# A streaming encoder layer on eight cores: later weights copied to bf16 in the first pass, third-pass buffers laid over early freed ones, engine orders from forward and backward list schedules

## The chip, the cores and the metric

The kernel runs on the 8 cores of one Trainium2 chip. Every core works on its own share of the data: half of one prompt stream (4096 rows), a halo of 128 rows before it, and 64 rows of new frames of running streams. The cores do not talk to each other. The metric is the device time of the slowest core, in microseconds (us). Repeated executions agree within a few tenths of a per cent, except in a second, slower state, in which some executions of any 8-core program fall. Engine names: PE is TensorE (PEld its weight loads), DVE is VectorE, ACT is ScalarE, POOL is GpSimd, and SP issues DMAs. PSUM (`PS` in the traces) is where this kernel's matmuls write; it is used as 8 banks.

## The reference, cut to what matters

```python
def encoder_layer(x, ...):
    x = x + 0.5 * swiglu_ffn(x, g_ff1, w_ff1_in, w_ff1_out)     # first pass  ("A" in the traces)
    z = rms_norm(x, g_mix) @ w_in                               # second pass ("B")
    cv, cg, q, k, v = split(z)
    c_out = conv_tail(history + cv * sigmoid(cg), w_dw, ...)    # causal depthwise conv, layer norm, swish
    a_out = attention(rope(norm(q)), rope(norm(k)), v, sinks)   # own chunk and the two before
    x = x + concat(c_out, a_out) @ w_out
    x = x + 0.5 * swiglu_ffn(x, g_ff2, w_ff2_in, w_ff2_out)     # third pass  ("C")
```

The model width is 1024, the hidden width of both feed-forward blocks 2816 (22 tiles of 128). All weights arrive as float32.

## The kernel before

The kernel records all its operations in program order together with what they read and write (on-chip buffers in pieces of 64 bytes, PSUM in banks), derives the dependencies, and lets a small scheduler choose an order for each engine. Each engine then runs its list strictly in order; semaphores enforce the dependencies. A dependency follows program order: if two operations use one buffer, the one recorded first goes first, and no scheduler can turn that round.

The scheduler before is greedy: an engine takes, among its next 24 operations, the first that is ready.

```python
WINDOW = {"sync": 24, "scalar": 24, "vector": 24, "gpsimd": 24, "tensor": 24}
def pick(e):
    ...                                  # cut: walks the engine's queue from its head
        if r <= f: return (f, u)         # the first one in program order that is ready
```

First and third pass are the same class: blocks of 384 rows; an up-projection writes `H`, a down-projection reads it. Weights are cast from float32 by the DMA itself.

```python
self.WU = C([128, NJ, 2048], BF16, "wu")     # lowest addresses: up weights, then down weights,
self.WD = C([128, NJ, 1024], BF16, "wd")     # then H, normed rows (XNT), rows (XA, XR) ...
def load_w(self, j): self.O.dma("gpsimd", ..., self.WU[:, j, :], self.wu[j])      # float32 -> bf16
def prologue():
    step = conv_weights(K, A.wd_off + 15 * 2048)   # its buffers lie over the last down weights
    for j in range(NJ): A.load_w(j)
    for g in range(16): step(g)                    # VectorE builds, a DMA stores: 16 x 288 KB
    for j in range(NJ): A.load_d(j)
```

The second pass runs in steps of 128 rows. This is the program order of a step, with the PSUM banks that each part uses:

```python
for n in range(last_step):
    flush_late()                              # ends normalization of step n-1's q, k (writes QN)
    if proj: self.glu_pe(n); self.glu_act(n)  # banks 0, 1
    if att:  self.transp(trq, ...)            # bank 6: q, k of step n-1 transposed
    ...                                       # cut: statistics, GLU product, convolution (banks 6, 7)
    if att:  self.scores(n - 1, 0)            # banks 2, 3, then an exponential on ScalarE
    if att:  self.scores(n - 1, 1)            # banks 4, 5
    if proj: self.qkv_pe(..., (self.pb[2], self.pb[3]))    # banks 2, 3: q, k, v of step n
    if att:  self.pv(n - 1)                   # banks 4, 5
    if proj: trq, f = self.qkv_post(n, ...)   # square, reduce, scale, rotate: ScalarE and VectorE
    ...                                       # cut: output projection of step n-22 (banks 0, 1)
```

## Time and profile before

The median is 2823.14 us. From the page of the slowest core: the busy time of the engines, then 40 equal slices of the span, each digit the busy tenths of a slice; PEclk is the granted TensorE clock and DMA the share of the 16 DMA engines.

```profile
PE 2492.3 (88%) x14740; PEld 1365.4 (48%) x14740; DVE 1032.1 (37%) x2701; ACT 747.9 (27%) x1303; POOL 216.3 (8%) x380
PE   1699999999999998888688962469999999999998
PEclk9899999999999998899799986779999999999999
DMA  9931222112221163223244559862111221111110
```

TensorE is full, except at the start, in the second pass (about slices 16 to 23) and in a deep hole after it. The windows view of the same execution, cut at four events: the end of the first pass's last down matmul, the last attention matmul, the first down matmul of the third pass, and the end. Columns: stretch and length, busy time of PE, PEld, DVE, ACT and POOL with instruction counts, granted clock, DMA share, GB/s.

```profile
0.00:1090.90 1090.90, 1000.79 (x5900) 557.97 (x5901) 405.90 (x1199) 257.50 (x445) 87.21 (x145) 0.98 0.34 86
1090.90:1612.10 521.20, 434.14 (x2747) 218.14 (x2744) 272.38 (x620) 263.38 (x451) 52.75 (x97) 0.91 0.35 98
1612.10:1911.00 298.90, 160.87 (x922) 91.36 (x919) 110.77 (x271) 68.10 (x110) 58.74 (x105) 0.77 0.74 180
1911.00:2817.90 906.90, 896.50 (x5181) 497.88 (x5179) 243.04 (x611) 158.91 (x297) 17.64 (x33) 1.00 0.15 50
```

I call these stretches first pass, inside of the second pass, transition, and rest. TensorE is idle for 90 us, nearly all at the start, then 87, 138 and 10 us. What TensorE waited for (six of its waits in the whole execution; total us, times, longest):

```profile
PE PS L343 <- DVE A_sm L343: 62.6, 2, 36.1
PE PS L343 <- DVE B_mc_145 L343: 51.0, 2, 30.1
PE PS L343 <- DVE B_x_128 L343: 32.9, 3, 26.2
PE PS L343 <- DVE B_qn L343: 28.9, 15, 4.0
PE PS L343 <- DVE B_qkt L343: 21.4, 17, 7.0
PE PS L343 <- DVE C_xb L343: 14.9, 3, 7.8
```

The first is the start (VectorE's row norms). The second and third are the transition: the transposed convolution output `B_mc` and the output buffers `B_x`. The next two are short waits for normed and transposed q and k inside the second pass. The last is for the third pass's own row norms. The chain of waits shows why the transition is long: small DMAs take 25 us while the third pass's float32 weights stream in (start, length, what).

```profile
1736.39 25.41 DMA B_mt_161<-zd
1768.94 26.77 DMA x<-B_x_128
```

### The profile page before, as it was taken

How to read it: one execution, taken by the hardware profiler on the slowest of the kernel's cores; microseconds unless marked ns; L12 is line 12 of the kernel's file. 1: busy time of each engine (PE TensorE's matmuls, PEld its weight loads, DVE VectorE, ACT ScalarE, POOL GpSimd, SP SyncE). 2: the span in 40 equal slices, each digit the busy share in tenths (PEclk: the TensorE clock that was granted, in tenths of full speed). 3: DMA queues.
4: the chain of work that ended last, by engine and by line, in shares of the span. 5: the costliest groups of instructions: out<-in, count | busy, mean ns of one | idle time of the engine just before them, and what ended most of it. 6: DMA issues, size and time to landing. Idle time of an engine off the chain costs nothing.

```text
span 2817.9 us, 41303 instructions; the slowest of 8 cores (2803.6 to 2817.9 us)
## 1 busy us (share of the span) xinstructions
PE 2492.3 (88%) x14740; PEld 1365.4 (48%) x14740; DVE 1032.1 (37%) x2701; ACT 747.9 (27%) x1303; POOL 216.3 (8%) x380
## 2 busy tenths in 40 slices
PE   1699999999999998888688962469999999999998
PEld 0345555555555554334344530145555555555554
DVE  2243443334433333544647562143223332233211
ACT  1112222222222222545546440031112211122110
POOL 2110000000000011000111123110000000000000
PEclk9899999999999998899799986779999999999999
DMA  9931222112221163223244559862111221111110
GB/s 199 165 94 55 76 79 64 47 48 79 87 64 42 38 159 74 55 57 105 68 132 115 184 169 217 197 145 64 45 53 38 68 68 52 53 40 52 46 45 23
DMA packets 111521, 244.00 MB, mean 87 GB/s; under 512 B 32415, under 2 KB 49695, under 8 KB 111319
## 3 DMA queue, kind: packets, MB, share of 16 engines
q0 software_dynamic: 42592, 131.65, 18.4%
q1 hardware_dynamic: 68727, 109.70, 13.5%
q8 instruction: 121, 1.98, 0.3%
q14 instruction: 81, 0.66, 0.1%
HBM read 207.82 MB, written 74.79 MB: 100 GB/s over the span
## 4 chain that ended last, share of the span: by engine, by line
PE 81%; DMA 9%; DVE 4%; issue 3%; ACT 2%; POOL 0%; SPq 0%; DVEq 0%; POOLq 0%; ACTq 0%
PE PS L343 81%; DMA wdc<-W_wb 3%; DMA x<-B_x_128 1%; DMA W_ey<-eye 1%; DMA B_mt_161<-zd 1%; DMA B_mt_160<-zd 1%; DVE B_y L343 1%; DMA C_wu<-wu 0%; ACT B_pt L343 0%; DMA B_x_128<-x 0%; DMA C_xa<-x 0%; DVE W_wb L343 0%; DMA B_hc<-sconv 0%; DVE B_qn L343 0%; ACT B_sq L343 0%
## 5 line engine op out<-in xcount | busy, mean ns | idle before, releaser
L343 PE MATMUL PS<-A_xnt,A_wu 128*128 128x384 bf16 (+1 forms) x3872 | 652.8, 330 | 0.9 <-ACT A_xnt L343 0.9
L343 PE MATMUL PS<-C_xnt,C_wu 128*128 128x384 bf16 (+1 forms) x3872 | 628.5, 324 | 0.8 <-ACT C_xnt L343 0.8
L343 PEld LDWEIGHTS PS<-A_xnt,A_wu 128*128 128x128 bf16 x3872 | 378.0, 98 | 258.1 <-issue 6.4
L343 PEld LDWEIGHTS PS<-C_xnt,C_wu 128*128 128x128 bf16 x3872 | 378.2, 98 | 240.5 <-issue 1.4
L343 PE MATMUL PS<-A_wd,A_h 128*128 128x512 bf16 (+1 forms) x1496 | 329.3, 381 | 5.0 <-DMA A_wd<-wd 5.0
L343 PE MATMUL PS<-C_wd,C_h 128*128 128x512 bf16 (+1 forms) x1452 | 315.3, 379 | 0.0
L343 ACT ACTIVATE C_sa<-PS 128x384 f32<-128x384 f32 (+1 forms) x242 | 117.5, 485 | 706.3 <-PE PS L343 696.0
L343 DVE TENSOR_TENSOR C_h<-PS,C_sa 128x384 bf16<-128x384 f32 (+1 forms) x242 | 133.3, 551 | 345.9 <-PE PS L343 345.1
L343 DVE TENSOR_TENSOR A_h<-PS,A_sa 128x384 bf16<-128x384 f32 (+1 forms) x242 | 136.0, 563 | 308.4 <-PE PS L343 307.6
L343 ACT ACTIVATE A_sa<-PS 128x384 f32<-128x384 f32 (+1 forms) x242 | 119.7, 495 | 430.2 <-PE PS L343 379.9
L343 PEld LDWEIGHTS PS<-A_wd,A_h 128*128 128x128 bf16 (+1 forms) x1496 | 146.7, 98 | 179.4 <-issue 9.1
L343 PEld LDWEIGHTS PS<-C_wd,C_h 128*128 128x128 bf16 (+1 forms) x1452 | 142.4, 98 | 169.9 <-issue 0.4
L343 DVE SCALAR_TENSOR_TENSOR C_xr<-PS,C_xr 128x512 f32<-128x512 f32 (+1 forms) x66 | 45.6, 691 | 281.3 <-PE PS L343 281.3
L343 PE MATMUL PS<-B_xn,B_wi 128*128 128x512 bf16 x512 | 126.5, 398 | 8.5 <-DVE B_t_76 L343 3.4
L343 PE MATMUL PS<-K_t,A_xb 128*128 128x128 bf16 (+1 forms) x544 | 42.9, 224 | 84.1 <-DVE A_sm L343 62.6
L343 PE MATMUL PS<-B_us,B_wr 128*128 128x256 bf16 (+1 forms) x576 | 88.2, 309 | 30.2 <-DVE B_qkt L343 17.6
L343 DVE SCALAR_TENSOR_TENSOR A_xr<-PS,A_xr 128x512 f32<-128x512 f32 (+1 forms) x68 | 46.9, 690 | 163.3 <-PE PS L343 163.1
L343 PE MATMUL PS<-B_wi,B_xn 128*128 128x256 bf16 (+1 forms) x512 | 92.6, 335 | 8.3 <-ACT B_pt L343 8.3
L343 PE MATMUL PS<-B_wo,B_mc_145 128*128 128x512 bf16 x64 | 20.7, 453 | 83.0 <-DVE B_mc_145 L343 51.0
L343 ACT ACTIVATE A_xb<-A_xr 128x1024 bf16<-128x1024 f32 (+1 forms) x34 | 35.8, 1053 | 201.5 <-DVE A_xr L343 201.5
L387 POOL DMA_DIRECT2D yout<-C_xr x33 | 17.6, 535 | 928.2 <-DVE C_xr L343 928.2
L343 ACT ACTIVATE B_pt<-PS 128x1024 bf16<-128x1024 f32 (+1 forms) x68 | 66.1, 984 | 78.6 <-PE PS L343 78.6
(167 smaller groups left out, 2029.4 us busy)
## 6 DMA issues: line engine op xcount, KB each, us to landing
B_wr<-wdc SPq DMA_DIRECT2D x32, 576.0 KB, 5.0
A_xa<-xin SPq DMA_DIRECT2D x33, 512.0 KB, 3.9
A_xr<-xin SPq DMA_DIRECT2D x33, 512.0 KB, 3.6
x<-A_xr POOLq DMA_DIRECT2D x33, 512.0 KB, 3.0
C_xr<-x SPq DMA_DIRECT2D x32, 512.0 KB, 3.7
C_xa<-x SPq DMA_DIRECT2D x32, 512.0 KB, 3.7
yout<-C_xr POOLq DMA_DIRECT2D x32, 512.0 KB, 2.9
A_wu<-wu POOLq DMA_DIRECT2D x22, 512.0 KB, 37.1
```

Of the source, the lines that this page charges most:

```text
L343: o = self.P.add(eng, lambda e: getattr(e, meth)(**kw), r, w, cost=self.cost(eng, meth, kw))
L387: self.P.add(eng, lambda e: e.dma_start(out=out, in_=in_), r, w, lane=lane, rk=rk, wk=wk, cost=1.0 if eng == "gpsimd" else 0.5, nbytes=n * ...
```

## The change

The intent is to close the holes around TensorE by four parts:

1. **Convolution steps moved.** VectorE's building of the convolution weights and their stores leave the start; 32 half-sized steps are spread over the first pass.
2. **Copies.** In the first pass, while DMA is idle, 60 DMAs copy all later weights from float32 to bf16 within DRAM. Later loads then read half the bytes, and can use the sync queue.
3. **Layout.** The third pass's rows, normed rows and `H` and 11 of its 22 up-weight tiles lie over projection and attention buffers, which end early. The other 11 lie over the convolution's. PSUM banks of up- and down-projection are exchanged so that up-projections avoid the banks of the output projection.
4. **List schedule.** The whole program is scheduled forward, with priorities from a backward schedule, in three rounds; the best by its own model is kept.

```diff
-    def schedule(self):                      # greedy, window of 24
+    def schedule(self, rounds=3):
+        def run(before, after, prio, back):  # list schedule over all units, by priority (cut)
+        for i in range(rounds):
+            start, order, t = run(preds, succs, prio, False)
+            if best is None or t < best[0]: best = (t, order)
+            start, _, _ = run(succs, preds, [-(start[u] + cost[u]) for u in range(n)], True)
+            prio = [-(start[u] + cost[u]) for u in range(n)]
...
+        fits = NJ if low is None else (low - c1.off) // 4096
+        self.WU = [(c1 if j < fits else c2)([128, 2048], BF16, "wu") for j in range(NJ)]
-        self.PU = [K.pb[0], K.pb[1], K.pb[2], K.pb[3]]
-        self.PD = [K.pb[4], K.pb[5]]
+        self.PU = [K.pb[2], K.pb[4], K.pb[3], K.pb[5]]
+        self.PD = [K.pb[0], K.pb[1]]
...
+    def hook(bi, j):                         # called in the first pass's up-projection
+        if bi == 0: return
+        if j % 3 == 1 and casts:
+            t, k, dst, src = casts.pop(0)
+            O.dma("gpsimd", "pc%d" % (k % 4), dst, src, wk=[("pc", t, k)], after=P.last["vector"])
+        if j % 5 == 3 and convs: wstep[0](*convs.pop(0))
...
-            O.dma("gpsimd", "bwi%d" % k, self.WI[:, k, :], d.wi[k])
+            O.dma("sync", "bwi%d" % k, self.WI[:, k, :], d.wib[k], rk=[("pc", "wi", k)])
...
-    Cc = FF(K, base, "C", d.wu2, d.wd2, ...)
+    Cc = FF(K, (c0, c0, c2), "C", d.wu2b, d.wd2b, ..., low=M.mid, weng="sync")
```

More of the change, by code (lines that the diff above doesn't have):

```diff
@@ L1 @@
+from heapq import heappush, heappop
 import numpy as np
@@ L15 @@
 SEM_MAX = 30000
+MARGIN = 0.5
+SLACK = 2
 ES = {F32: 4, BF16: 2, I32: 4}
 ATOM = 64
-WINDOW = {"sync": 24, "scalar": 24, "vector": 24, "gpsimd": 24, "tensor": 24}
 class _Op:
@@ L38, in __init__ @@
         self.order = None
+        self.last = {}
+        self.trace = []
     def sbuf(self, name, shape, dt, offset):
@@ L79, in atoms, with add @@
         return r
-    def add(self, eng, fn, reads=(), writes=(), lane=None, rk=(), wk=(), cost=0.1, nbytes=0):
+    def add(self, eng, fn, reads=(), writes=(), lane=None, rk=(), wk=(), cost=0.1, nbytes=0, after=None):
         o = _Op()
@@ L118, in add @@
             rd[k] = {}
+        if after is not None:
+            raw.add(after)
         if lane is not None:
@@ L125, in add @@
         weak.discard(o.idx)
+        self.last[eng] = o.idx
         o.deps = raw | weak
@@ L143, in units @@
         return out
-    def schedule(self):
+    def schedule(self, rounds=3):
         ops, units = self.ops, self.units()
         n = len(units)
-        deps = [set() for _ in range(n)]
+        preds = [set() for _ in range(n)]
         for u, l in enumerate(units):
             for o in l:
-                deps[u].update(ops[d].unit for d in o.deps)
-            deps[u].discard(u)
-        users = [[] for _ in range(n)]
-        left = [len(d) for d in deps]
-        for u, d in enumerate(deps):
+                preds[u].update(ops[d].unit for d in o.deps)
+            preds[u].discard(u)
+        succs = [[] for _ in range(n)]
+        for u, d in enumerate(preds):
@@ L157, in schedule @@
             for x in d:
-                users[x].append(u)
+                succs[x].append(u)
         eng = [l[0].eng for l in units]
-        queue = {e: [u for u in range(n) if eng[u] == e] for e in ENGS}
-        head = {e: 0 for e in ENGS}
-        free = {e: 0.0 for e in ENGS}
-        ready = [0.0] * n
-        done = [False] * n
-        pipe = 0.0
-        order, starts = [], []
-        cand = {}
-        def pick(e):
-            q, h = queue[e], head[e]
-            while h < len(q) and done[q[h]]:
-                h += 1
-            head[e] = h
-            best, bt, seen = None, None, 0
-            f = free[e]
-            while h < len(q) and seen < WINDOW[e]:
-                u = q[h]
-                h += 1
-                if done[u]:
-                    continue
-                seen += 1
-                if left[u]:
-                    continue
-                r = ready[u]
-                if r <= f:
-                    return (f, u)
-                if bt is None or r < bt - 0.05:
-                    best, bt = u, r
-            return None if best is None else (bt, best)
@@ L191, in schedule @@
-        dirty = set(ENGS)
-        for _ in range(n):
-            for e in dirty:
-                cand[e] = pick(e)
-            e = min((x for x in ENGS if cand[x] is not None), key=lambda x: cand[x][0])
-            t, u = cand[e]
-            done[u] = True
-            cost = sum(o.cost for o in units[u])
-            free[e] = end = t + cost
-            if units[u][0].lane is not None:
-                pipe = max(pipe, end + 0.5) + units[u][0].nbytes / 230e3
-                end = max(pipe, end + 1.5) + 0.3
-            order.append(u)
-            starts.append(t)
-            dirty = {e}
-            for x in users[u]:
-                left[x] -= 1
-                lat = 0.06 if eng[x] == e else 0.16
-                if ready[x] < end + lat:
-                    ready[x] = end + lat
-                if not left[x]:
-                    dirty.add(eng[x])
@@ L213, in schedule, with release, pick @@
-        self.order = [o for u in order for o in units[u]]
-        self.model_us = max(free.values())
+        cost = [sum(o.cost for o in l) for l in units]
+        dma = [l[0].lane is not None for l in units]
+        wire = [l[0].nbytes / 250e3 if d else 0.0 for l, d in zip(units, dma)]
+        def run(before, after, prio, back):
+            left = [len(x) for x in before]
+            ready = [0.0] * n
+            free = {e: 0.0 for e in ENGS}
+            wait, now = {e: [] for e in ENGS}, {e: [] for e in ENGS}
+            start = [0.0] * n
+            order = []
+            pipe = 0.0
+            def release(u):
+                heappush(wait[eng[u]], (ready[u], prio[u], u))
+            def pick(e):
+                f, w, r = free[e], wait[e], now[e]
+                while w and w[0][0] <= f + 1e-9:
+                    _, p, u = heappop(w)
+                    heappush(r, (p, u))
+                if r:
+                    return f
+                return w[0][0] if w else None
+            for u in range(n):
+                if not left[u]:
+                    release(u)
+            cand = {e: pick(e) for e in ENGS}
+            for _ in range(n):
+                e = min((x for x in ENGS if cand[x] is not None), key=lambda x: cand[x])
+                t = cand[e]
+                if now[e]:
+                    u = heappop(now[e])[1]
+                else:
+                    u = heappop(wait[e])[2]
+                start[u] = t
+                order.append(u)
+                end = free[e] = t + cost[u]
+                if dma[u] and not back:
+                    pipe = max(pipe, end + 0.5) + wire[u]
+                    end = max(pipe, end + 1.5) + 0.3 + SLACK
+                dirty = {e}
+                for x in after[u]:
+                    left[x] -= 1
+                    lat = 0.06 if eng[x] == e else 0.16 + (MARGIN if back else 0.0)
+                    if back and dma[x]:
+                        lat += 2.0 + SLACK + wire[x]
+                    if ready[x] < end + lat:
+                        ready[x] = end + lat
+                    if not left[x]:
+                        release(x)
+                        dirty.add(eng[x])
+                for x in dirty:
+                    cand[x] = pick(x)
+            return start, order, max(free.values())
@@ new lines, in schedule @@
+        prio = list(range(n))
+        best = None
+        for i in range(rounds):
+            start, order, t = run(preds, succs, prio, False)
+            if best is None or t < best[0]:
+                best = (t, order)
+            start, _, _ = run(succs, preds, [-(start[u] + cost[u]) for u in range(n)], True)
+            prio = [-(start[u] + cost[u]) for u in range(n)]
+            self.trace.append(t)
+        self.order = [o for u in best[1] for o in units[u]]
+        self.model_us = best[0]
@@ L379, in tr, with dma @@
         self.op("tensor", "transpose", out=out, in_=in_, identity=identity)
-    def dma(self, eng, lane, out, in_, rk=(), wk=()):
+    def dma(self, eng, lane, out, in_, rk=(), wk=(), after=None):
         r = [in_] if in_.tensor.name in self.P.info else []
@@ L387, in dma @@
         self.P.add(eng, lambda e: e.dma_start(out=out, in_=in_), r, w, lane=lane, rk=rk, wk=wk,
-                   cost=1.0 if eng == "gpsimd" else 0.5, nbytes=n * max(ES[in_.dtype], ES[out.dtype]))
+                   cost=1.0 if eng == "gpsimd" else 0.5, nbytes=n * max(ES[in_.dtype], ES[out.dtype]), after=after)
 class Carve:
@@ L422, with __init__ @@
 class FF:
-    def __init__(self, K, off, tag, wu, wd, g1, g2, blocks, src, dst, xnd=None, rkey=None, wkey=None, nkey=None):
+    def __init__(self, K, carves, tag, wu, wd, g1, g2, blocks, src, dst, xnd=None, rkey=None, wkey=None, nkey=None, low=None, cwd=None, weng="gpsimd", hook=None):
         self.K, self.O, self.tag = K, K.O, tag
@@ L430, in __init__ @@
         self.rkey, self.wkey, self.nkey = rkey, wkey, nkey
-        C = Carve(K.P, off, tag)
         nmax = max(sum(n for _, n in b) for b in blocks)
-        self.WU = C([128, NJ, 2048], BF16, "wu")
-        self.wd_off = C.off
-        self.WD = C([128, NJ, 1024], BF16, "wd")
-        self.H = C([128, NJ, nmax], BF16, "h")
-        self.XNT = [C([128, 8, nmax], BF16, "xnt") for _ in range(2)]
-        self.XA = [C([128, D], F32, "xa") for _ in range(2)]
-        self.XR = [C([128, D], F32, "xr") for _ in range(3)]
-        self.XB = [C([128, D], BF16, "xb") for _ in range(2)]
-        self.XO = [C([128, 8, 128], BF16, "xo") for _ in range(2)] if g2 is not None else None
-        self.SA = [C([128, nmax], F32, "sa") for _ in range(2)]
-        self.G1 = C([128, D], F32, "g1")
-        self.G2 = C([128, D], F32, "g2") if g2 is not None else None
-        self.SM = C([128, 8, 16], F32, "sm")
-        self.end = C.off
+        self.weng, self.hook = weng, hook
+        c0, c1, c2 = carves
+        self.XA = [c0([128, D], F32, "xa") for _ in range(2)]
+        self.XNT = [c0([128, 8, nmax], BF16, "xnt") for _ in range(2)]
+        self.XB = [c0([128, D], BF16, "xb") for _ in range(2)]
+        self.G1 = c0([128, D], F32, "g1")
+        self.SM = c0([128, 8, 16], F32, "sm")
+        self.SA = [c0([128, nmax], F32, "sa") for _ in range(2)]
+        self.H = c0([128, NJ, nmax], BF16, "h")
+        fits = NJ if low is None else (low - c1.off) // 4096
+        self.WU = [(c1 if j < fits else c2)([128, 2048], BF16, "wu") for j in range(NJ)]
+        c3 = c0 if cwd is None else cwd
+        self.WD = c3([128, NJ, 1024], BF16, "wd")
+        self.XR = [c3([128, D], F32, "xr") for _ in range(3)]
+        self.XO = [c3([128, 8, 128], BF16, "xo") for _ in range(2)] if g2 is not None else None
+        self.G2 = c3([128, D], F32, "g2") if g2 is not None else None
         self.cnt = dict(xa=0, xr=0, xb=0, xo=0, sm=0, ab=0, d=0, t=0)
         self.g1, self.g2 = g1, g2
-        self.PU = [K.pb[0], K.pb[1], K.pb[2], K.pb[3]]
-        self.PD = [K.pb[4], K.pb[5]]
+        self.PU = [K.pb[2], K.pb[4], K.pb[3], K.pb[5]]
+        self.PD = [K.pb[0], K.pb[1]]
         self.PT = [K.pb[6], K.pb[7]]
@@ L465, in load_w @@
     def load_w(self, j):
-        self.O.dma("gpsimd", self.tag + "wu%d" % (j % 8), self.WU[:, j, :], self.wu[j])
+        k = [("pc", self.tag + "u", j)] if self.weng == "sync" else []
+        self.O.dma(self.weng, self.tag + "wu%d" % (j % 8), self.WU[j][:, :], self.wu[j], rk=k)
     def load_d(self, j):
-        self.O.dma("gpsimd", self.tag + "wd%d" % (j % 8), self.WD[:, j, :], self.wd[j])
+        k = [("pc", self.tag + "d", j)] if self.weng == "sync" else []
+        self.O.dma(self.weng, self.tag + "wd%d" % (j % 8), self.WD[:, j, :], self.wd[j], rk=k)
     def load_xa(self, g):
@@ L542, in up @@
             a, b = self.PU[i], self.PU[2 + i]
-            W = self.WU[:, j, :].rearrange("p (k n) -> p k n", k=8)
+            W = self.WU[j][:, :].rearrange("p (k n) -> p k n", k=8)
             for h, ps in ((0, a), (1, b)):
@@ L551, in up @@
             bg(1)
+            if self.hook:
+                self.hook(bi, j)
             if j == 10:
@@ L673, in __init__ @@
         self.V = [C([128, 128], BF16, "v") for _ in range(4)]
+        self.PT = [C([128, 2, 512], BF16, "pt") for _ in range(3)]
+        self.DN = [C([128, 512], F32, "dn") for _ in range(2)]
+        self.mid = C.off
         self.WO = C([128, 8, 1024], BF16, "wo")
@@ L688, in __init__ @@
         self.KS, self.VSO = self.KO, self.VO
-        self.PT = [C([128, 2, 512], BF16, "pt") for _ in range(3)]
-        self.DN = [C([128, 512], F32, "dn") for _ in range(2)]
         self.WR = [C([128, 2, 1152], BF16, "wr") for _ in range(2)]
@@ L745, in setup @@
         for k in range(8):
-            O.dma("gpsimd", "bwo%d" % k, self.WO[:, k, :], d.wo[k])
+            O.dma("sync", "bwo%d" % k, self.WO[:, k, :], d.wob[k], rk=[("pc", "wo", k)])
         O.memset(self.CN[:, 0:1], EPS)
@@ L992, in load_wd @@
         self.O.dma("sync", "bwr%d" % i, self.WR[i][:, :, :], self.d.wdc[2 * q:2 * q + 2].rearrange("g p n -> p g n"),
-                   rk=[("wdc", 2 * q), ("wdc", 2 * q + 1)])
+                   rk=[("wdc", g, h) for g in (2 * q, 2 * q + 1) for h in range(2)])
     def conv_pe(self, t, q, half):
@@ L1284, in window_out_prompt, with conv_weights, step @@
         O.dma("sync", "bpv", d.ovw_p[:, :], self.VO[:, :])
-def conv_weights(K, off):
+def conv_weights(K, C, buf):
     P, O, d = K.P, K.O, K.d
-    C = Carve(P, off, "W")
-    CO = C([128, 16, 36], F32, "co")
-    EY = C([128, 32], F32, "ey")
-    WB = [C([128, 36, 32], BF16, "wb") for _ in range(2)]
-    O.dma("sync", "wco", CO[:, :, :], d.wcoef)
-    O.dma("sync", "wey", EY[:, :], d.eye32)
-    def step(g):
-        w = WB[g % 2]
-        O.tt(w[:, :, :], EY[:, :].unsqueeze(1).to_broadcast([128, 36, 32]), CO[:, g, :].unsqueeze(2).to_broadcast([128, 36, 32]), ALU.mult)
-        O.dma("gpsimd", "wdc%d" % (g % 2), d.wdc[g], w[:, :, :].rearrange("p a b -> p (a b)"), wk=[("wdc", g)])
+    CO = C([128, 16, 36], BF16, "co")
+    EY = C([128, 32], BF16, "ey")
+    O.dma("gpsimd", "wco", CO[:, :, :], d.wcoef)
+    O.dma("gpsimd", "wey", EY[:, :], d.eye32)
+    def step(g, h):
+        w = buf()[:, :, :].rearrange("p a b -> p (a b)")[:, 0:576]
+        O.tt(w.rearrange("p (a b) -> p a b", b=32), EY[:, :].unsqueeze(1).to_broadcast([128, 18, 32]),
+             CO[:, g, 18 * h:18 * h + 18].unsqueeze(2).to_broadcast([128, 18, 32]), ALU.mult)
+        O.dma("gpsimd", "wdc%d" % h, d.wdc[g][:, 576 * h:576 * h + 576], w, wk=[("wdc", g, h)])
     return step
@@ L1330, in build_nc @@
     dram("wdc", [16, 128, 1152], BF16)
+    dram("wib", [8, 128, 1792], BF16)
+    dram("wob", [8, 128, D], BF16)
+    dram("wu2b", [NJ, 128, 2048], BF16)
+    dram("wd2b", [NJ, 128, D], BF16)
     dram("ud", [512, 4, 1032], BF16)
@@ L1354, in xnd @@
         return d.xne[:, :, g[0] - HALF:g[0] - HALF + g[1]]
-    A = FF(K, base, "A", d.wu1, d.wd1, d.gains[0], d.gains[1], [main[0:2] + [halo, samp]] + b3, d.xin, d.x1,
-           xnd=xnd, wkey=lambda g: [("x1", g[0])], nkey=lambda g: [("xn", g[0] // 128)])
+    cu = Carve(P, base, "A")
+    cr = Carve(P, base + NJ * 4096, "A_")
+    casts = [("wi", k, d.wib[k], d.wi[k]) for k in range(8)] + [("wo", k, d.wob[k], d.wo[k]) for k in range(8)]
+    for j in range(NJ):
+        casts += [("Cu", j, d.wu2b[j], d.wu2[j]), ("Cd", j, d.wd2b[j], d.wd2[j])]
+    convs = [(g, h) for g in range(16) for h in range(2)]
+    def hook(bi, j):
+        if bi == 0:
+            return
+        if j % 3 == 1 and casts:
+            t, k, dst, src = casts.pop(0)
+            O.dma("gpsimd", "pc%d" % (k % 4), dst, src, wk=[("pc", t, k)], after=P.last["vector"])
+        if j % 5 == 3 and convs:
+            wstep[0](*convs.pop(0))
+    A = FF(K, (cr, cu, cu), "A", d.wu1, d.wd1, d.gains[0], d.gains[1], [main[0:2] + [halo, samp]] + b3, d.xin, d.x1,
+           xnd=xnd, wkey=lambda g: [("x1", g[0])], nkey=lambda g: [("xn", g[0] // 128)], hook=hook)
+    wstep = [None]
     def loads(F):
@@ L1367, in prologue @@
     def prologue():
-        step = conv_weights(K, A.wd_off + 15 * 2048)
-        for j in range(NJ):
-            A.load_w(j)
-        for g in range(16):
-            step(g)
-        for j in range(NJ):
-            A.load_d(j)
+        loads(A)()
+        wstep[0] = conv_weights(K, cr, lambda: A.XO[A.nxt("xo", 2)])
     A.run(prologue)
+    assert not casts and not convs
     M = Mixer(K, base)
@@ L1379, in build_nc @@
     M.run()
-    Cc = FF(K, base, "C", d.wu2, d.wd2, d.gains[2], None, [main[0:2] + [samp]] + b3, d.x2, d.yout, rkey=lambda g: [("x2", g[0])])
+    c0 = Carve(P, base, "C")
+    c2 = Carve(P, M.US_off, "C_")
+    Cc = FF(K, (c0, c0, c2), "C", d.wu2b, d.wd2b, d.gains[2], None, [main[0:2] + [samp]] + b3, d.x2, d.yout, rkey=lambda g: [("x2", g[0])],
+            low=M.mid, weng="sync")
+    assert c0.off <= M.US_off
     Cc.run(loads(Cc))
@@ L1383, in build_nc @@
     with ExitStack() as st:
-        print(P.model_us, P.emit(st), A.end, M.end, Cc.end)
+        print(P.model_us, P.emit(st), cr.off, M.mid, M.US_off, M.end, c0.off, c2.off)
     return nc
```

## The prediction

> **What bounds it now.** By the slowest core's page TensorE is busy 2492 of 2818 us; the chain of waits is 81% TensorE. The windows view shows 100% busy at clock 1.00 from 216 to 1092 us (first pass, blocks 1 to 10) and from 1883 to 2808 us (third pass). The loss is elsewhere:
>
> 1. Start, 0 to 216 us: 126 us busy. Block 1 starts at 216.6 us. DMA is 97% busy to 62 us with float32 weights cast on the way. VectorE stands in order behind the convolution-weight steps, which wait for their buffers' stores (27.6 us at one time), and TensorE behind VectorE's norm (36 and 26.6 us). Those buffers lie over the last down weights.
> 2. First to second pass, 1092 to 1118 us: some 15 us.
> 3. Second pass, 1108 to 1660 us: 456 busy of 552 us, clock 0.91; many short waits.
> 4. Second to third pass, 1660 to 1858 us: 75 busy of 198 us, clock 0.69, DMA share 0.84. Two waits on the transposed convolution output (51 us) and three on output buffers (33 us); the chain shows small loads of 25 to 27 us beside 34 MB of float32 weights, issued from 1715 us on.
>
> **What the change does.** (1) The convolution steps leave the start: 4.7 MB of stores (about 24 us at the 197 GB/s measured there) and VectorE's stalls go. Weights are down by 110 to 125 us; the third and fourth row tiles still land at about 50 us, so block 0's up-projection (22 x 3.03 us) runs from 62 to 130 us, its down-projection (8 x 4.7 us) to 168 us. Gain 48 us. (2) The 60 DRAM casts (46 MB read, 23 MB written) go where DMA share is 0.24 and TensorE full: free, as are the small VectorE steps. (3) The second pass's input weights come as bf16 by the sync queue: gain 12 us. The Trainium skill, "DMA: Bandwidth & Descriptors", section "SWDGE vs HWDGE vs iDMA", says a cast during DMA is for the gpsimd queue only, so the copies permit this. (4) List scheduling over the whole program instead of a window of 24 should halve the loss inside the second pass: 45 us. (5) Largest: the third pass's activations and 11 of 22 up-weight tiles lie where projection and attention buffers end, and its PSUM banks avoid the output projection's, so its norms and half of block 0's up-projection (23 us) fill the second pass's tail. All down weights still wait for the last output projections: I leave 40 us. Gain 120 us.
>
> **Sum.** First pass ends at 168 + 876 = 1044 us, second starts at 1049; TensorE work of the second at full clock about 485 us (estimate from the first pass's rate), of the third 945 us; losses 50 inside the second, 40 at the transition, 10 at the end, 5 between profile and median: about 2585 us, 8.5% faster.
>
> Prediction 2585 us, 2510 to 2680. Faster by over 2%: 0.95; within: 0.035; slower: 0.015.
>
> **What would show it.** Block 1's first up matmul at 155 to 185 us; first pass 876 us from there; third-pass matmuls among the second's; TensorE idle between last attention and full third pass below 70 us, not 123.
>
> **What would make it wrong.** Orders tuned to a model whose DMA latencies are too short: in-order queues then stall, chiefly sync with weight loads ahead of small ones; casts delaying stores whose buffers the convolution steps share, so VectorE blocks.

## The result, and the profile after

The changed kernel takes 2675.66 us (median of 4, 2675.11 to 2678.91), the kernel before 2823.14 us. The ratio is 0.9482 (95% interval 0.9463 to 0.9500): 5.2% faster. A ratio here is the mean time of one kernel's fast runs over that of the other's fast runs of the same rounds, so not quite the ratio of the medians quoted. The time lies inside the predicted range, at its upper edge, and 91 us above the predicted value. So the change worked, but some 40% of the expected gain is missing, and the question is which part.

The page's lines after:

```profile
PE 2485.1 (93%) x14740; PEld 1367.4 (51%) x14740; DVE 1030.0 (38%) x2717; ACT 764.4 (29%) x1311; POOL 224.7 (8%) x398
PE   1999999999999999798869976799999999999998
PEclk9999999999999999898879988899999999999999
DMA  9943444345433344122235685750121112110110
```

The first slices are fuller and the hole after the second pass is shallower. The second pass (again about slices 16 to 23) looks much as it did. The windows view, cut at the same four events:

```profile
0.00:1053.60 1053.60, 995.90 (x5883) 555.73 (x5884) 402.30 (x1201) 256.40 (x439) 119.01 (x209) 1.00 0.48 111
1053.60:1570.50 516.90, 446.86 (x2875) 232.30 (x2874) 301.86 (x705) 287.50 (x486) 54.16 (x98) 0.91 0.41 115
1570.50:1779.90 209.40, 154.17 (x881) 86.88 (x882) 88.64 (x226) 65.61 (x99) 33.87 (x59) 0.85 0.67 217
1779.90:2677.20 897.30, 888.20 (x5111) 492.48 (x5107) 237.18 (x585) 154.90 (x289) 17.62 (x33) 1.00 0.15 50
```

First pass 37 us shorter, inside of the second pass **4 us**, transition 90 us, rest 10 us (TensorE has 8 us less to do in it: some work had moved ahead): 141 us, the whole difference of the two profiled spans.

The 4 us are a poor measure of the new order, because the stretch ends with the last attention matmul and a scheduler may put that off. The 166 transposes of q and k, the same in both kernels, show it (count, ns, first and last start in us):

```profile
L343 PE MATMUL PS<-K_t,B_qn x166: 188/219/314, 1116.4 to 1603.3; 128*128 128x128 bf16 x161, 64*128 64x64 bf16 x5
L363 PE MATMUL PS<-K_t,B_qn x166: 190/219/314, 1076.2 to 1520.4; 128*128 128x128 bf16 x161, 64*128 64x64 bf16 x5
```

From the first to the last they take 487 us before and 444 us after, with some 110 fewer matmuls of other work between them; but the last attention matmul follows the last transpose by 9 us before and by 50 us after. The stretch after holds 128 more matmuls than the one before. The fairest figure for the order's gain inside is therefore TensorE's idle time, which falls from 87 to 70 us: 17 us. Three waits of TensorE in the inside and the transition:

```profile
PE PS L363 <- DVE B_qn L363: 26.8, 10, 4.3
PE PS L363 <- DVE C_xb L363: 19.8, 2, 10.6
PE PS L363 <- DVE B_mc_164 L363: 9.9, 2, 5.9
```

The 25 us DMAs are gone from the chain of waits, and the waits on `B_mc` fall from 51 to 10 us. The wait for `B_qn` is nearly as it was (26.8 against 28.9 us), that for `B_qkt` falls from 21.4 to 8.1 us. The wait for the third pass's own row norms (`C_xb`), 15 us before, is 20 us now.

Why does the second pass not shorten more? The chain of waits after, at one step (start, length, what):

```profile
1373.61 7.14 PE PS L363 x40
1380.83 0.71 ACT B_sq L363
1381.63 0.82 DVE B_qs L363
1382.45 0.73 DVE B_t_94 L363
...
1384.87 0.83 DVE B_qn L363
1385.83 0.45 PE PS L363 x5
1386.38 0.50 DVE B_qkt L363
1387.01 7.08 PE PS L363 x38
1394.18 0.71 ACT B_sq L363
```

In this step it is a closed loop, 13.4 us from one `B_sq` to the next. TensorE computes scores, then the next projection; ScalarE squares it; VectorE reduces, scales and rotates; TensorE transposes (`x5`); VectorE copies (`B_qkt`); then come the next scores. Scores and projection share PSUM banks 2 and 3, and the program records scores of step n-1 ahead of the projection of step n. So the projection cannot start before these scores are read, and the scores need the end of the previous projection's whole post-processing. The TensorE timeline before shows a similar beat, from its transposes of `B_qn` (start, length, what; in brackets the idle time just before and what ended it):

```profile
1285.74 0.44 PE L343 MATMUL PS<-K_t,B_qn 128*128 128x128 bf16 x5
1299.33 0.44 PE L343 MATMUL PS<-K_t,B_qn 128*128 128x128 bf16 x5
1313.52 0.44 PE L343 MATMUL PS<-K_t,B_qn 128*128 128x128 bf16 x5 [0.37 <-DVE B_qn L343]
```

Before 13.6 to 14.2 us a step; but there TensorE has more work in a step, and two of these three transposes do not wait. After:

```profile
1372.42 0.44 PE L363 MATMUL PS<-K_t,B_qn 128*128 128x128 bf16 x5 [2.83 <-DVE B_qn L363]
1385.83 0.44 PE L363 MATMUL PS<-K_t,B_qn 128*128 128x128 bf16 x5 [1.82 <-DVE B_qn L363]
1399.24 0.69 PE L363 MATMUL PS<-K_t,B_qn 128*128 128x128 bf16 x5 [3.27 <-DVE B_qn L363]
```

In these steps the beat is 13.4 us, hardly less than before, although the list schedule had moved the gated convolution's projections (glu) elsewhere and they hold less work. It is no fixed bound: from 1160 us on, the steps of this trace take between 11.5 and 16.2 us, and in the step shown the exponential had read the scores by 1375.2 us while the projection began only at 1378.0 us, behind matmuls of the convolution and its statistics that the scheduler had put between. What no order can do is take the post-processing out of the loop. The Trainium skill, "Perfetto Trace Analysis", section "Optimization Strategy", says of such repeated equal gaps that they can mean that there isn't enough SBUF or PSUM for the next tile. This trace agrees in part: in these steps the gap of 2 to 3 us returns every 13.4 us, and the resource is a pair of PSUM banks; but the experiment below shows that it is the order of their users that counts here.

### The profile page after: what moved, and what is told of

The parts are those of the page before. It is cut to its first block, busy times and chain, and to the rows that moved or that the text cites. A ratio compares the mean times of both kernels' runs of the same rounds, so it can differ in the third digit from the quotient of the medians.

```text
span 2677.2 us, 41546 instructions; the slowest of 8 cores (2662.2 to 2677.2 us)
## 1 busy us (share of the span) xinstructions
PE 2485.1 (93%) x14740; PEld 1367.4 (51%) x14740; DVE 1030.0 (38%) x2717; ACT 764.4 (29%) x1311; POOL 224.7 (8%) x398
## 4 chain that ended last, share of the span: by engine, by line
PE 85%; DMA 7%; DVE 4%; issue 2%; ACT 1%; DVEq 0%; POOL 0%; ACTq 0%; POOLq 0%; SPq 0%
PE PS L363 85%; DMA A_wd<-wd 4%; DVE B_y L363 1%; DMA B_wr<-wdc 1%; DMA xnt<-A_xo 0%; DMA A_wu<-wu 0%; DMA B_x_152<-x 0%; DVE B_qs L363 0%; DVE C_sm L363 0%; DMA C_xa<-x 0%; ACT B_sq L363 0%; DVE B_t_94 L363 0%; DVE B_qn L363 0%; ACT B_se L363 0%; DMA x<-B_x_152 0%
## 5 line engine op out<-in xcount | busy, mean ns | idle before, releaser
L363 PEld LDWEIGHTS PS<-B_us,B_wr 128*128 128x128 bf16 x576 | 60.2, 109 | 46.6 <-issue 27.2
L363 PEld LDWEIGHTS PS<-B_xn,B_wi 128*128 128x128 bf16 x512 | 48.5, 100 | 61.8 <-issue 15.1
```

The costliest lines, as they stand in the source:

```text
L363: o = self.P.add(eng, lambda e: getattr(e, meth)(**kw), r, w, cost=self.cost(eng, meth, kw))
```

## The experiments

All outputs are right. Medians are of all runs of a kernel; where slow runs are among them, the lowest stands in brackets. Stretches are from the profile of the slowest core. The kernel before took 2825.5 to 2834.3 us (medians) beside them. The runs come from three chips (old_sched, f32_weights, old_layout and only_sched; qkv_early, bf16_gpsimd and slack8; the other five), so differences of less than about 10 us between these groups are not firm. The border between inside and transition, the last attention matmul, moves with the order; read it together with the total.

| kernel | median us | ratio to before | first pass | inside | transition | rest |
|---|---|---|---|---|---|---|
| before | 2823.1 | 1 | 1090.9 | 521.2 | 298.9 | 906.9 |
| changed | 2675.7 | 0.9482 | 1053.6 | 516.9 | 209.4 | 897.3 |
| old_sched | 2740.8 | 0.9682 | 1051.8 | 516.5 | 263.2 | 905.1 |
| f32_weights | 2730.1 | 0.9647 | 1054.2 | 516.1 | 259.2 | 898.8 |
| old_layout | 2728.5 (2727.3) | 0.9640 | 1055.6 | 509.4 | 255.0 | 905.6 |
| only_sched | 2787.2 (2786.7) | 0.9849 | 1091.0 | 508.4 | 280.3 | 905.6 |
| bf16_gpsimd | 2681.5 (2680.1) | 0.9494 | 1053.0 | 516.8 | 214.3 | 898.5 |
| slack8 | 2736.5 (2722.0) | 0.9670 | 1055.0 | 545.9 | 220.7 | 898.5 |
| qkv_early | 2625.7 (2622.0) | 0.9289 | 1053.4 | 470.4 | 202.9 | 897.2 |
| old_sched_qkv | 2677.5 (2676.6) | 0.9485 | 1053.0 | 455.7 | 261.0 | 905.2 |
| norm_late | 2615.8 | 0.9262 | 1053.3 | 474.2 | 191.5 | 897.4 |
| tiles_first | 2627.8 (2626.2) | 0.9302 | 1055.3 | 476.5 | 196.3 | 897.3 |
| late_slack1 | 2628.4 (2624.6) | 0.9272 | 1057.1 | 484.8 | 188.1 | 897.4 |
| late_slack4 | 2624.4 | 0.9268 | 1055.7 | 465.2 | 202.3 | 897.3 |

### What each part is worth

**old_sched: the changed kernel with the old scheduler.**

```diff
-    def schedule(self, rounds=3):     # list schedule
+    def schedule(self):               # the greedy one of the kernel before, window 24
```

> The changed kernel with the old greedy scheduler (window of 24 units) put back; copies, layout and moved convolution steps stay. Theory: the moved convolution steps alone make the start, so block 1's first up matmul stays at 165 to 185 us; without the list schedule the other gains shrink: first to second pass gap 10 us more, second pass inside 20 to 40 us longer, third-pass matmuls not mixed into the second pass's tail (window too short), so the transition costs 40 us more. Total about 2750 us. Rival: the copies and the layout do nearly all of it and the order little, total below 2700 us. If the start falls back beyond 200 us, the order and not the moved steps made the start.

Measured: 65 us slower than the changed kernel. The first pass stays at 1052 us, so the moved convolution steps made the start, not the order. The inside is the same to half a microsecond, 516.5 us, but this does not refute the theory's 20 to 40 us for it: by the weight loads counted there, the greedy order has 138 fewer matmuls in it, and its q and k transposes take 490 us from first to last, against 444 us. The transition is 54 us longer.

**f32_weights: no copies.**

```diff
-            O.dma("sync", "bwi%d" % k, self.WI[:, k, :], d.wib[k], ...)
+            O.dma("gpsimd", "bwi%d" % k, self.WI[:, k, :], d.wi[k])      # likewise wo, wu2, wd2
+    casts = []
```

> The changed kernel without the bf16 copies: no casts in the first pass, the later weights are read as float32 and cast on the gpsimd queue as before. Theory: first pass unchanged within 5 us (copies are free there); first to second pass gap 10 us longer; transition 15 to 30 us longer because twice the bytes are read where DMA is at 0.7 to 0.9. Total about 2705 us. Rival: the halved bytes are what shortened the transition, then total above 2740 us. If the copies were not free in the first pass, it gets shorter than 881 us here.

Measured: 54 us slower, 50 of them in the transition. This is above my estimate of 15 to 30 us; the total lies between the theory's 2705 us and the rival's 2740 us, nearer to the rival. The first pass is 1054.2 us without copies and 1053.6 us with them: the 60 copies are free there. The second pass does not start later with float32 input weights (inside 516.1 us), so the predicted gain of 12 us at that border does not exist.

**old_layout: the third pass's buffers in the old places.**

```diff
-    Cc = FF(K, (c0, c0, c2), "C", ..., low=M.mid, weng="sync")
+    Cc = FF(K, (c0, c1, c1), "C", ..., cwd=cw, weng="sync")   # c1: bottom, cw above it, c0 on top
```

> The changed kernel with the third pass's buffers laid out as before (up weights at the bottom, then down weights, activations on top); everything else stays. Theory: layout plus whole-program order make the overlap; here activations lie over buffers that live to the end of the second pass, so no third-pass matmul runs before the last output projection or shortly before, and the transition costs 50 to 70 us more: about 2735 us. Rival: layout is of little use because the last output projections bound the transition anyway: below 2700 us. The first pass and the second up to the last attention step stay as in the changed kernel.

Measured: 53 us slower; the transition takes 46 us more. The first up matmul of the third pass starts at 1767 us, after the last output projection at 1726 us; in the changed kernel it starts at 1635 us, 105 us before the last one. As the theory expected. The exchange of the PSUM banks stayed in this run; what it is worth alone was not tested.

**only_sched: the kernel before with the new scheduler alone.**

```diff
-    def schedule(self):               # greedy
+    def schedule(self, rounds=3):     # list schedule
```

> The kernel before with only the scheduler exchanged. Theory: the start stays late (the convolution steps' stores still compete for DMA and their buffers lie under the last down weights; block 1 at 195 to 215 us), the second pass gains 30 to 40 us inside, the transition stays long with float32 loads (100 us or more idle): total about 2765 us. Rival: the order is most of the change: below 2720 us.

Measured: 36 us faster than before by the medians, 1.5% by the ratio. (Its interval, 0.9784 to 0.9913, leaves it open whether that is 2%.) The first pass stays at 1091 us, the inside shortens by 13 us and the transition by 19 us. Order alone helps little where buffers and bytes are in the way.

Taken together: in the transition, taking away any one of order, copies and layout loses 46 to 54 us of the 90 us gained, and order alone gives 19 us (for the order, part of it belongs to the inside, since the order moves the border). The three need each other; their parts do not add up.

**bf16_gpsimd: copies kept, but loaded by the other queue.**

```diff
-            low=M.mid, weng="sync")
+            low=M.mid, weng="gpsimd")       # still from wu2b, wd2b
```

> The changed kernel with the copies kept, but the third pass's bf16 weights loaded by the gpsimd queue instead of the sync queue. Without copies the transition (last attention matmul to first third-pass down matmul) took 259 us, with them 209. Theory bytes: half the bytes make the difference, so it stays at 210 to 220 us, total 2675 to 2690 us. Rival queue: what counts is that the loads leave the gpsimd queue, where they wait in order with the stores and small loads of the tail, then 240 us or more, total above 2710 us.

Measured: 2681.5 us, transition 214 us. Of the 50 us which the copies are worth there, 5 come from the queue of the third pass's weights (less than is firm between groups of runs) and some 45 remain for the bytes. A load of float32 is also cast on the way, and the runs do not separate the halved bytes from the missing cast.

### Why the second pass did not shorten

**qkv_early: the projection recorded ahead of the previous step's scores.**

```diff
+            prev = trq
+            if proj:
+                self.qkv_pe(..., (self.pb[2], self.pb[3]))
+                trq, f = self.qkv_post(n, ...)
...
             if att:
-                self.transp(trq, 128, self.QKT[n % 4])
+                self.transp(prev, 128, self.QKT[n % 4])
...
-            if proj: self.qkv_pe(..., (self.pb[2], self.pb[3]))      # was here, behind the scores
-            if proj: trq, f = self.qkv_post(n, ...)
```

No instruction is added or removed; only who goes first on banks 2 and 3 changes.

> The changed kernel with one edit in the second pass's program: a step's q, k, v projection (and its post-processing) is emitted ahead of the previous step's scores, which share PSUM banks 2 and 3 with it, instead of behind them. Theory: the list schedule did not shorten the second pass (517 against 521 us from its start to the last attention matmul) because the program order of the two users of these banks closes a loop of 13.4 us per step (projection, square, reduce, scale, transpose, scores, exponential, next projection) that no order can break; with the edit the loop loses the square-to-transpose part, 5 to 6 us, steps become bound by TensorE at about 11 to 12 us, this stretch falls to 450 to 475 us, the whole to 2615 to 2640 us. Rival: the stretch is bound by in-order queues or by the low granted clock of 0.91, then it stays above 505 us and the total at 2665 to 2685 us.

Measured: 2625.7 us, 50 us faster than the changed kernel; inside 470.4 us. The wait for `B_qn` is gone from the longest waits, and in its most even steps the transposes follow each other at 11.4 us (mean over all steps 12.4 us, against 14.3 us in the changed kernel and 15.7 us in the one before). From the TensorE timeline:

```profile
1229.55 0.45 PE L363 MATMUL PS<-K_t,B_qn 128*128 128x128 bf16 x5
1240.94 0.46 PE L363 MATMUL PS<-K_t,B_qn 128*128 128x128 bf16 x5
```

and the windows view of the inside:

```profile
1053.40:1523.80 470.40, 428.34 (x2891) 225.92 (x2890) 304.60 (x708) 285.69 (x489) 53.38 (x99) 0.95 0.46 130
```

From 1150 to 1250 us TensorE is now busy all the time at clock 1.00: these steps are bound by it, as the theory had it. TensorE's idle time inside falls from 70 to 42 us, and its busy time for about the same work from 447 to 428 us, because the granted clock rises from 0.91 to 0.95. The rival, a bound by queues or by the clock itself, is refuted: the stretch fell well below its 505 us, and the clock rose as the idle time fell. (Giving the projection other banks, instead of the other order, was not tried.)

**old_sched_qkv: the same edit with the old greedy scheduler.**

```diff
-    def schedule(self, rounds=3):     # list schedule
+    def schedule(self):               # greedy, window 24; with the edit of qkv_early
```

> The early projection with the old greedy scheduler (window of 24). With the old program order the two schedulers took 516 us each from the end of the first pass to the last attention matmul. Theory: the loop over banks 2 and 3 was the bound for either, so here too this stretch falls, to 470 to 495 us, total 2695 to 2720 us. Rival: only the whole-program order can use the freedom, then it stays above 508 us, total above 2730 us.

Measured: inside 455.7 us (516.5 before the edit), even below the expected band, total 2677.5 us. The edit is worth 63 us in total with the greedy scheduler and 50 us with the list schedule: the loop held both back. With this edit of a few lines the old scheduler is as fast as the changed kernel with its new one. With the edit in both, the list schedule is still 52 us ahead in total. The stretches put all of this into the transition, but the list schedule's q and k transposes also take less time from first to last (386 against 422 us), so part of it is won inside.

### The transition

**slack8: the scheduler's model with a larger allowance per DMA.**

```diff
-SLACK = 2
+SLACK = 8
```

> The changed kernel with the model's allowance per DMA raised from 2 to 8 us. Theory: TensorE stands 26 us in the transition (1587 to 1626 us) behind a weight load of the convolution and behind third-pass norms whose row loads came later than the model had them; with a larger allowance these waits shrink by half or more, total 2655 to 2668 us. Rival: the waits come from order on VectorE and ScalarE, not from DMA latencies: within 5 us of the changed kernel, or slower.

Measured: 61 us *slower* by the medians, 29 of them inside the second pass and 11 in the transition by the profiled run, which is one of the quicker ones. Both the theory and its rival's "within 5 us" are wrong in size; the rival's "or slower" is right. In the transition the wait for `C_xb` stays at 19.6 us. A larger allowance makes the schedule worse and does not touch this wait.

What the wait is can be seen on VectorE's timeline of qkv_early, which has the same pattern:

```profile
1553.03 0.42 DVE L363 TENSOR_SCALAR B_lm<-PS 128x256 f32<-128x256 f32 x1 [0.87 <-PE PS L363]
...
1567.90 0.67 DVE L363 TENSOR_SCALAR C_sm<-C_sm 128x1 f32<-128x1 f32 x3 [4.16 <-ACT C_xb L363]
...
1573.45 0.42 DVE L363 SCALAR_TENSOR_TENSOR B_lr<-PS,B_se 128x256 f32<-128x256 f32 x1
```

`B_lm` and `B_lr` are mean and variance of the second pass's last layer norm, on the way to its last outputs. They need the same PSUM bank and could follow each other, but between them stand two of the third pass's row norms, the second of which waits for its rows: 20 us.

**norm_late: the third pass's first rows loaded only behind that layer norm** (on top of qkv_early).

```diff
+        self.ln_op = O.P.last["scalar"]                     # at the end of ln_head
...
-        self.O.dma("sync", ..., self.XA[i][0:n, :], ...)
+        self.O.dma("sync", ..., self.XA[i][0:n, :], ..., after=self.xa_after if g in self.blocks[0] else None)
```

> On the kernel with the early projection (2625.7 us): the row loads of the third pass's first block may only be issued after the last layer norm's statistics of the second pass (its reciprocal root on ScalarE). Theory: in the transition VectorE stands in order in three third-pass norms (1558 to 1572 us) whose rows come late, behind which the last layer norm's statistics wait 20 us (TensorE idle 19 us there); with the norms behind them the last output projection, at 1684 us, comes 15 to 20 us earlier and the total is 2605 to 2615 us. Rival: the norms are needed soon after, so the wait only moves to the third pass's start: total within 6 us of 2626 us.

Measured: 2615.8 us, transition 191.5 instead of 202.9 us. TensorE's wait for `C_xb` falls from 19.0 to 2.5 us, but that for the output buffers rises from 9.3 to 14.5 us, and `B_lr` still comes 12 us behind `B_lm` (1553.7 and 1566.1 us), now with a load of `B_mt` ahead of it. The last output projection comes only 6 us earlier (1677.9 against 1684.2 us), not 15 to 20. So the wait was real, but much of the expected gain is taken over by the next waits. The total, 10 us lower, just misses the expected band; the two kernels ran on different chips and their intervals overlap, so the gain itself is not firm: only the vanished wait is.

**tiles_first: all four row tiles of the first block loaded at once** (on top of qkv_early).

```diff
+        if self.hook:
+            for k, (r, n) in enumerate(rest):               # tiles 3 and 4 into the output-row buffers
+                self.xa[(r, n)] = self.XR[k]
+                self.O.dma("sync", ..., self.XR[k][0:n, :], ...)
```

> On the kernel with the early projection: the third and fourth row tile of block 0 in the first pass are loaded at once into buffers that are free then, instead of into the first two tiles' buffers after their norm. Theory: the start is bound by the float32 weights (block 0's first down matmuls wait for their last tiles at 134 to 137 us, DMA share 0.98), so although the up-projection begins at about 30 instead of 58 us, the first pass ends only 0 to 10 us earlier: total 2615 to 2626 us. Rival: TensorE's late begin sets the time, then the gain is 20 to 28 us.

Measured: no gain, 2627.8 us. The first up matmul starts at 33.5 instead of at about 58 us (57.65 us in the changed kernel), but then TensorE stops for its weights:

```profile
33.50 29.78 PE L363 MATMUL PS<-A_xnt,A_wu 128*128 128x448 bf16 x144 [0.94 <-ACT A_xnt L363]
112.91 8.14 PE L363 MATMUL PS<-A_xnt,A_wu 128*128 128x448 bf16 x32 [9.12 <-DMA A_wu<-wu]
```

The first pass ends at 1055.3 us. What is left of the start is bound by the float32 weights, as expected.

**late_slack1 and late_slack4: norm_late with the allowance at 1 and 4 us.**

```diff
-SLACK = 2
+SLACK = 1        # and 4
```

> The best kernel so far (2615.8 us) with the model's allowance per DMA at 1 instead of 2 us. Raising it to 8 us had cost 61 us in the changed kernel, half of it inside the second pass. Theory: the list schedule is a lottery in a parameter that the chip does not have; small steps move it by 5 to 20 us either way, without a trend, and the first pass does not move. Rival: the cost rises steadily with the allowance, so 1 us gives 2600 to 2612 us.

> The same at 4 us. Theory (lottery): 2600 to 2640 us, sign unknown. Rival (steady cost): about 20 us slower, 2630 to 2640 us, all of it between the first pass and the third.

Measured: ratios 0.9272 and 0.9268, against 0.9262 at 2 us: no trend, as the "lottery" had it. The inside falls by 20 us (484.8, 474.2, 465.2 us for 1, 2, 4) while the transition grows by 14 us (188.1, 191.5, 202.3 us): mostly the border between them moves. So the large loss at 8 us in the changed kernel is no steady cost of the allowance at small values; what made 8 us bad was not followed up.

The best version is norm_late: 2615.8 us, ratio 0.9262, that is 7.4% faster than before and 60 us below the changed kernel (some 50 us of it firm, from qkv_early).

## Why the prediction was right or wrong

Right: the direction, the range (2675.66 us in 2510 to 2680, by 4 us), and where the two largest gains come from (points 1 and 5). The value was 91 us too low. That the time still fell inside the range is owed to its width, not to the sum: one point failed and one term was missing, and 5 us more would have left it. Point by point:

1. *The convolution steps leave the start, gain 48 us.* Right in mechanism; the gain is 37 us (first pass 1090.9 to 1053.6 us). Block 1's first up matmul came at 171.85 us (predicted 168). What I missed is that the kernel before had already done 48 of block 1's up matmuls, about 8 us of work, before the 216.6 us that I read as its start. only_sched (1091.0 us) shows that order does not do it; old_sched, f32_weights and old_layout (1051.8 to 1055.6 us) show that it needs neither the order nor the copies nor the third pass's layout. What is left is the moved steps, together with the first pass's own new layout and order of loads; these were not separated.
2. *Copies are free in the first pass.* Right: 1053.6 us with, 1054.2 us without.
3. *Input weights as bf16, gain 12 us.* Wrong: 0. f32_weights starts and runs the second pass as fast. The chain of waits before shows a load of the convolution's history (`B_hc`, 8.8 us) at that border, not the weights; I put the gap down to the load that the change happened to touch. The Trainium skill, "DMA: Bandwidth & Descriptors", section "SWDGE vs HWDGE vs iDMA", was used rightly (a casting DMA must go by the gpsimd queue, so the copies permit the change of queue), but bf16_gpsimd shows that the queue is worth 5 us in the transition and the bytes, or the missing cast, 45.
4. *The list schedule "should halve the loss inside the second pass: 45 us".* **This is the step that failed**: the stretch is 4 us shorter, and TensorE's idle time in it falls by 17 us, from 87 to 70 us, where the sum left 50 us. I took the short waits for bad order alone. Behind them is a loop closed by program order over PSUM banks 2 and 3 (13.4 us in the steps shown), which an order can fill but not open; opening it took 50 us off the total with the list schedule and 63 us with the greedy one.
5. *Layout, PSUM banks and early start of the third pass, gain 120 us.* Right in mechanism (third-pass matmuls from 1635 us, among the output projections); transition and rest together gained 99 us. TensorE's idle time in the transition fell from 138 to 55 us; 20 us of what is left is the wait for `C_xb`, which the prediction's last paragraph had named as a risk, though on the sync queue, whereas it is VectorE that stands in order.

The sum has one more mis-sized term. I counted the second pass's TensorE work at full clock, 485 us, and added idle time only. In the changed kernel TensorE is *busy* 446.9 + 154.2 + 888.2 = 1489 us after the first pass, against the 1430 us in the sum: 59 us. An estimate from the granted clock agrees: 446.9 x (1 - 0.91) + 154.2 x (1 - 0.85) = 63 us. Idle time in inside and transition was 125 us, against 90 us. The second pass starts 5 us later than in the sum (1053.6 against 1049 us). These three make 99 us; the end and the allowance between profile and median were 7 us smaller together than I had put them, and I had rounded up by 1 us: that leaves the 91 us that were missing.

## What to carry to other kernels

Before expecting anything of a better order, look for a beat in the trace: if the same gap returns at a fixed period, follow the chain once round, find the buffer or PSUM bank that closes it, and ask which of its two users the program names first. Changing that is a few lines and here gained 50 us, more than the 17 us of idle time that the new order took out of the second pass. When two orders are compared by stretches, do not end a stretch with an event that an order can put off, or count the work in it as well: here it hid part of the scheduler's gain. Overlap of two phases needs order, free buffers and spare bytes together, so test such parts by taking one away at a time, not only by adding one. And in a phase with gaps, count TensorE's work at the clock that it is granted there.

## What the Trainium skill lacked or had wrong

- "TensorE: Matmul & The Clock Gate", "What's actually happening": it says that the array runs at half clock after an idle window of about 3.4 us. Seen in the timeline after: 18 convolution matmuls take 2.14 us in full flow and 4.00 us behind a wait of 6.43 us. But shorter gaps did it too: nine of them took 1.16 us at 1363.5 us and 2.10 us at 1374.0 us, behind waits of 2.83 and 0.74 us with only five transposes between.

```profile
1580.51 2.14 PE L363 MATMUL PS<-B_us,B_wr 128*128 128x256 bf16 x18
1593.25 4.00 PE L363 MATMUL PS<-B_us,B_wr 128*128 128x256 bf16 x18 [6.43 <-DMA B_wr<-wdc]
```

  The same section puts the ramp penalty at less than 1% of a typical kernel's span; it speaks of the ramp at a kernel's start. It is no figure for a kernel that loses the clock again and again: here the loss is 63 us of 2677 us by the estimate above, 2.4%, 40 us of it inside the second pass and 23 us in the transition.
- "Perfetto Trace Analysis", "Optimization Strategy": its sentence on repeated gaps names missing PSUM as a cause, but as a matter of buffer count and tile sizes. Here neither was changed: exchanging the program order of two users of the same two banks took 50 us off the total (inside 516.9 to 470.4 us).
- "DMA: Bandwidth & Descriptors", "Issuing engine by pattern": it calls loads issued from the sync queue generally faster than those from the gpsimd queue. No run here shows that for single loads: in the crowded transition the 512 KB weight loads landed in 8.2 us (median) by the sync queue and in 7.4 us by the gpsimd queue, and the whole kernel was 6 us slower with the latter.
- None of the pages that I read says what casting copies within DRAM cost beside a busy TensorE: 60 of them (46 MB read) left the first pass at 1053.6 us, against 1054.2 us without them.
